# State space input tiles turned during the gated embedding and scaled by the norm afterwards, tables loaded early from ScalarE's queue

## The chip, the cores and the metric

One core of one Trainium2 chip runs the whole kernel in one launch. The metric is device time in microseconds (us); the kernel before is shown by the median of 3 runs and by one profiled execution. TensorE (PE, with its weight loads PEld), VectorE (DVE), ScalarE (ACT), GpSimd (POOL) and SyncE (SP) each work through their own instructions in a fixed order. SP and ScalarE also issue the DMAs of this kernel. The built program counts the landings of these DMAs on eight semaphores in turn, so that an issue also waits until the DMA eight places ahead of it has landed, and what stands behind it on its engine waits too.

## The reference, cut to what matters

Two transformer blocks on x of 512 tokens by 1024 channels. The change lies in the first one, between the gated embedding of layer 0 and the state space mixer of layer 1:

```python
# layer 0, end: gated embedding
gate = sigmoid(rms_norm(x) @ ple_w_gate[0])
x = x + gate * (p[0] @ ple_w_proj[0])
# layer 1, begin: state space mixer over 64 groups of 16 channels, 64 complex states each
h = rms_norm(x, norm_mix[1])                 # x * rsqrt(mean(x*x) + eps) * g
y = s5_mixer(h, ...)                         # input map, complex linear scan over time, output map, + d*h
g_a, g_b = split(gelu(y) @ od_w_glu, 2)
x = x + g_a * sigmoid(g_b)
```

## The kernel before, in words

The kernel keeps x turned, channels on partitions: eight tiles x0 to x7 of 128 channels by 512 tokens. A matmul in fp32 precision is made of three (lines 354 to 356 in `mm_fm`): high half of the weights by high and low half of the input, low half by high half. Weights arrive as 1 MB tiles `raw` (`fetch`, line 310, SP) and are split into `whi` (ScalarE, line 328) and `wlo` (VectorE or GpSimd, line 331).

**The gated embedding** (`ple`, line 872) goes over four weight tiles of two channel tiles each (c = 0 to 3). For each finished tile m it forms the gate (line 933 on ScalarE) and adds to x[m] (lines 934, 935), then calls `done(m)`: here `Rms.add`, a square on ScalarE (line 218) and a sum over tiles. It also multiplies out the projection of layer 1's embedding ahead of time and stores it to HBM (`ahead_of_time`, lines 897 and 902). At the end, `Rms.fin1` sums over channels on TensorE (line 202), forms 1/sqrt on ScalarE and VectorE (`rstd_of`, line 174) and a diagonal matrix (line 189); `Rms.fin2` spreads it over partitions by a matmul with ones (line 196) and ScalarE copies it into a tile `st_r` (line 197). The projection's last two tiles stand between `fin1` and `fin2`.

**The state space mixer** (from line 1192) works on eight units, one per channel tile. It handles the scan in blocks of 4 tokens, so each unit needs its input with channel and token phase on the partitions. For that `drive` (line 1215, VectorE) multiplies x[k] by gain and norm into a tile `h` (two buffers), ScalarE's queue stores it to HBM (`hd`, line 1217), and `lift` reads it back turned, in four DMAs on SP (`up`, line 1223). `load` (line 1210, SP) brings a unit's tables from HBM in six DMAs: `tG` (input map), `tE` (rotations) and `tC` (output map), two buffers each. Then, per unit: `mid` has 8 matmuls `tG` by `up` into two banks (line 1230) and six VectorE products and sums with `tE` (lines 1233 to 1238; called the rotation here); `scan` has two VectorE scans (line 1249) and five or six GpSimd products and sums with `tE` (lines 1256 to 1262; of odd units the difference `xr`, line 1258, is VectorE's); `emit` has 12 matmuls with `tC` (line 1270), a gelu on ScalarE (line 1272), a store to `hd` (line 1273, ScalarE's queue) and four loads that turn it back (`y`, line 1277, SP); `land` splits y into `Gh` (ScalarE, line 291) and `Gl` (VectorE, line 294), the input of the gated linear unit behind it. That unit has eight groups (c = 0 to 3 with two halves s = 1, 0) of 48 matmuls. The group c = 0, s = 1 (`acc0[1]`) is accumulated in the loop, unit by unit; c = 0, s = 0 (`acc0[0]`) stands behind the loop.

A loop over t (line 1293) staggers the units: `load` of t+1, `mid` of t, `scan` of t-1, `land` of t-3, `emit` of t-2, `acc0[1]` of t-4. A scheduler then sets the order of the instructions on each engine by what is ready when; the order in which things stand in a section below is that of the built program. SP's order there is: tables of unit 0, tG of unit 1, lifts of unit 0, tE and tC of unit 1, then all 28 lifts of units 1 to 7, and only then the tables of unit 2.

Of the kernel before, what the change touches and what calls it, by code (L numbers as in the profile page):

```python
# [10 lines left out]
F32 = mybir.dt.float32  # L11
# [7 lines left out]
P = 128  # L19
# [30 lines left out]
def tile_net(ctx: ExitStack, tc: tile.TileContext, a, out):  # L50
# [1138 lines left out]
    rms2 = Rms()  # L1189
    rb2 = ple(0, X, rms, rms2.add, (rms2.fin1, rms2.fin2))  # L1190

    with tc.tile_pool(name="s5r", bufs=1) as rp:
# [5 lines left out]
        class Unit:  # L1198
# [4 lines left out]
            def load(self):  # L1203
                k = self.k
                self.G = rp.tile([P, 4, 256], F32, tag="tG", name=nm("tG"), bufs=2)
                self.E = rp.tile([P, 4, 256], F32, tag="tE", name=nm("tE"), bufs=2)
                self.C = rp.tile([P, 4, 448], F32, tag="tC", name=nm("tC"), bufs=2)
                for t, lo, hi in ((self.G, 0, 256), (self.E, 704, 960), (self.C, 256, 704)):
                    for i in range(2):
                        nc.sync.dma_start(t[:, 2 * i:2 * i + 2, :],  # L1210
                                          tabs[2 * k + i].rearrange("p (q n) -> p q n", q=2)[:, :, lo:hi])

            def drive(self):
                h = rp.tile([P, 4, P], F32, tag="h", name=nm("h"), bufs=2)
                vec.scalar_tensor_tensor(h, x[self.k].rearrange("p (n j) -> p j n", j=4), col("norm_mix", KD + self.k),
                                         rb2.rearrange("p (n j) -> p j n", j=4), op0=ALU.mult, op1=ALU.mult)
                nc.scalar.dma_start(hdr[self.k], h)

            def lift(self):
                self.up = rp.tile([P, 4, P], F32, tag=f"Gh{self.k}", name=nm("up"))  # L1220
                src = hdr[self.k].rearrange("(i c) j n -> j c i n", c=32)
                for b in range(4):
                    nc.sync.dma_start(self.up[32 * b:32 * b + 32], src[3 - b])

            def mid(self):
                k, up = self.k, self.up
# [12 lines left out]
                self.rm = xt_(f"X{'hl'[self.par]}5")  # L1239
                act.copy(self.rm, r4[:, 4 * k:4 * k + 4].unsqueeze(2).to_broadcast([P, 4, P]))  # L1240
                pool.memset(self.rm[:, :, 0:1], 0.0)

            def scan(self):
                k = self.k
                er, ei = self.E[:, :, 0:P], self.E[:, :, P:]
                zr = rp.tile([P, 4, P], F32, tag=f"Gl{k}", name=nm("zr"))
                zi = rp.tile([P, 4, P], F32, tag="zi", name=nm("zi"), bufs=2)
                for z, w in ((zr, self.pv[1]), (zi, self.pv[0])):
                    vec.tensor_tensor_scan(z.rearrange("p i n -> p (i n)"), self.rm.rearrange("p i n -> p (i n)"),
                                           w.rearrange("p i n -> p (i n)"), 0.0, op0=ALU.mult, op1=ALU.add)  # L1250
# [35 lines left out]
        for u in units:  # L1286
            u.drive()
# [537 lines left out]
```

## Time and profile before

| | |
|---|---|
| median of 3 runs | 2817.63 us (2815.61 to 2818.87) |
| the profiled execution | 2815.37 us |
| its span | 2813.6 us |
| PE busy, share of the span | 96% |
| chain that ended last | PE 86%, DVE 6%, POOL 2%, DMA 2%, ACT 2%, issue 2% |
| granted TensorE clock over the span | 0.981 |

Times within the profile are counted from the start of the span. The profiled execution lies 2.3 us below the median. A busy engine is one that executes; TensorE's matmuls overlap, so 96% is not a measure of how full it is. Waits are put down to the work whose semaphore came last.

### The profile page before, as it was taken

Reading aid. Unit: us, or ns where it says so; the run is one execution under the profiler, and the core shown is the slowest. Engines: PE = TensorE matmul, PEld = TensorE weight load, DVE = VectorE, ACT = ScalarE, POOL = GpSimd, SP = SyncE. Lnnn points to the kernel's source line nnn. Section 1 sums busy time; section 2 is a strip of 40 time slices with the busy share of each in tenths; the row PEclk is TensorE's granted clock in tenths of the full one; section 3 lists DMA queues with packets and bytes.
Section 4 is the critical chain, followed back from the end, with each engine's and each line's share of the span. In section 5 each row is a group of like instructions: output and inputs, shape, how many; then the busy total and the mean of one; then the engine's idle time right before and its main releaser. Section 6 shows DMA issues by size and latency. Waiting matters only on the chain.

```text
span 2813.6 us, 35122 instructions
## 1 busy us (share of the span) xinstructions
PE 2709.8 (96%) x14363; PEld 2293.3 (82%) x14363; DVE 1608.2 (57%) x2526; ACT 987.6 (35%) x1287; POOL 671.5 (24%) x590
## 2 busy tenths in 40 slices
PE   8999999999579999999999998999999899999998
PEld 8978888878468888888888887887888778889898
DVE  6456868676664746475333346965478664733335
ACT  5544424345223423244212234333343352431222
POOL 2213045761441000011000035344444321300000
PEclk9999999999789999999999999999999999999999
DMA  5203333433753232223232222232222223222222
GB/s 161 76 31 106 105 111 133 173 118 126 251 173 100 90 100 95 90 95 130 90 105 90 93 87 73 87 100 77 96 81 82 75 90 114 74 98 90 90 92 74
DMA packets 277842, 289.83 MB, mean 103 GB/s; under 512 B 20197, under 2 KB 266951, under 8 KB 277680
## 3 DMA queue, kind: packets, MB, share of 16 engines
q1 hardware_dynamic: 256208, 260.38, 28.9%
q10 hardware_dynamic: 20640, 26.78, 2.7%
q8 instruction: 113, 1.85, 0.3%
q0 software_dynamic: 832, 0.41, 0.1%
q14 instruction: 49, 0.40, 0.0%
HBM read 263.43 MB, written 24.12 MB: 102 GB/s over the span
## 4 chain that ended last, share of the span: by engine, by line
PE 86%; DVE 6%; POOL 2%; issue 2%; DMA 2%; ACT 2%; SPq 0%; POOLq 0%; DVEq 0%; ACTq 0%
PE ps L354 23%; PE ps L355 23%; PE ps L356 23%; PE ps L363 4%; PE ps L365 4%; PE ps L364 4%; DVE ps L1491 1%; PE ps L635 1%; PE ps L1552 1%; PE ps L659 1%; DVE x L287 1%; POOL st_b L263 1%; PE ps L1116 1%; DMA hd<-h 0%; ACT whi L328 0%
## 5 line engine op out<-in xcount | busy, mean ns | idle before, releaser
L328 ACT CAST whi<-raw 128x2048 fp32r<-128x2048 f32 (+2 forms) x216 | 406.2, 1881 | 763.4 <-PE ps L355 608.4
L354 PE MATMUL ps<-Xh,whi 128*128 128x512 f32 (+1 forms) x1472 | 571.3, 389 | 6.8 <-ACT Xh L291 5.1
L356 PE MATMUL ps<-Xh,wlo 128*128 128x512 f32 (+1 forms) x1472 | 566.3, 385 | 3.1 <-DVE wlo L331 3.1
L355 PE MATMUL ps<-Xl,whi 128*128 128x512 f32 (+1 forms) x1472 | 566.7, 385 | 2.7 <-POOL Xl L294 2.7
L331 DVE TENSOR_TENSOR wlo<-raw,whi 128x2048 fp32r<-128x2048 f32 (+2 forms) x167 | 381.0, 2281 | 324.1 <-ACT whi L328 320.2
L331 POOL TENSOR_TENSOR wlo<-raw,whi 128x2048 fp32r<-128x2048 f32 (+1 forms) x49 | 223.5, 4561 | 689.6 <-ACT whi L328 377.7
L354 PEld LDWEIGHTS ps<-Xh,whi 128*128 128x128 f32 x1472 | 278.7, 190 | 65.4 <-ACT Xh L291 5.5
L356 PEld LDWEIGHTS ps<-Xh,wlo 128*128 128x128 f32 x1472 | 279.2, 190 | 60.7 <-DVE wlo L331 4.4
L355 PEld LDWEIGHTS ps<-Xl,whi 128*128 128x128 f32 x1472 | 279.3, 190 | 59.5 <-POOL Xl L294 3.6
L355 PE MATMUL ps<-XBl,whi 128*128 128x512 f32 (+1 forms) x736 | 283.3, 385 | 2.6 <-POOL XBl L294 2.6
L354 PE MATMUL ps<-XBh,whi 128*128 128x512 f32 (+1 forms) x736 | 282.6, 385 | 1.4 <-ACT XBh L291 1.4
L356 PE MATMUL ps<-XBh,wlo 128*128 128x512 f32 (+1 forms) x736 | 282.5, 385 | 0.0
L355 PE MATMUL ps<-Al,whi 128*128 128x512 f32 (+1 forms) x528 | 203.7, 386 | 3.2 <-DVE Al L294 3.2
L354 PE MATMUL ps<-Ah,whi 128*128 128x512 f32 (+1 forms) x528 | 203.6, 388 | 1.2 <-ACT Ah L291 1.2
L356 PE MATMUL ps<-Ah,wlo 128*128 128x512 f32 (+1 forms) x528 | 203.5, 386 | 0.0
L1491 DVE SCALAR_TENSOR_TENSOR ps<-glu,par,ps 128x512 f32<-128x512 f32 x232 | 174.3, 751 | 4.2
L355 PEld LDWEIGHTS ps<-XBl,whi 128*128 128x128 f32 x736 | 139.8, 190 | 31.6 <-POOL XBl L294 3.4
L354 PEld LDWEIGHTS ps<-XBh,whi 128*128 128x128 f32 x736 | 139.4, 190 | 29.3 <-ACT XBh L291 1.8
L356 PEld LDWEIGHTS ps<-XBh,wlo 128*128 128x128 f32 x736 | 139.8, 190 | 28.0
L220 POOL TENSOR_TENSOR st_a<-st_a,st_q 128x512 f32<-128x512 f32 x25 | 44.3, 1770 | 487.9 <-ACT st_q L218 487.8
L363 PE MATMUL ps<-whi,Xh 128*128 128x256 f32 (+1 forms) x512 | 147.7, 289 | 0.7 <-ACT z L597 0.4
L364 PE MATMUL ps<-wlo,Xh 128*128 128x256 f32 (+1 forms) x512 | 145.0, 284 | 0.0
(472 smaller groups left out, 4869.7 us busy)
## 6 DMA issues: line engine op xcount, KB each, us to landing
raw<-in_ffn_w_up_dram SPq DMA_DIRECT2D x66, 1024.0 KB, 5.1
raw<-in_w_in_dram SPq DMA_DIRECT2D x40, 1024.0 KB, 5.2
raw<-in_ffn_w_down_dram SPq DMA_DIRECT2D x32, 1024.0 KB, 4.9
raw<-in_ffn_w_gate_dram SPq DMA_DIRECT2D x22, 1024.0 KB, 5.2
tab<-tabs ACTq DMA_DIRECT2D x16, 960.0 KB, 4.1
raw<-in_ffn_w_down_dram SPq DMA_DIRECT2D x16, 768.0 KB, 4.2
raw<-in_ev_w_in_dram SPq DMA_DIRECT2D x8, 1024.0 KB, 5.2
raw<-in_ple_w_gate_dram SPq DMA_DIRECT2D x8, 1024.0 KB, 4.9
```

What stands on the lines that cost most here:

```text
L220: eng.tensor_tensor(self.acc, self.acc, sq, op=ALU.add)
L263: eng.tensor_tensor(self.sq[:, c], self.sq[:, c], q[:, c], op=ALU.add)
L287: vec.tensor_tensor(xm, xm, self.rb[:, c], op=ALU.mult)
L328: cp = act.copy(hi, rv)
L331: lo.tensor_tensor(lw, rv, hi.bitcast(F32), op=ALU.subtract)
L354: pe.matmul(acc, wh[j][:, s], X.h[k], start=start and t == 0, stop=False)
L355: pe.matmul(acc, wh[j][:, s], X.l[k], start=False, stop=False)
L356: pe.matmul(acc, wl[j][:, s], X.h[k], start=False, stop=stop and t == len(ks) - 1)
L363: pe.matmul(acc, X.h[k][:, s], wh[j], start=start and t == 0, stop=False)
L364: pe.matmul(acc, X.h[k][:, s], wl[j], start=False, stop=False)
L365: pe.matmul(acc, X.l[k][:, s], wh[j], start=False, stop=stop and t == len(ks) - 1)
L1491: vec.scalar_tensor_tensor(x[m] if t == 30 else acc, u[:, t:t + T], col("ck", t * KD + m), acc, op0=ALU.mult, op1=ALU.add)
```

## The change

What it does:

- `turn_in(k)` runs from `ple`'s `done(m)`, as soon as x[m] is final: ScalarE multiplies x[k] by the gain alone (line 1220 of the new file), ScalarE's queue stores h, SP lifts it into `up`. The norm is applied afterwards: `phases` spreads the diagonal as `rbt`, one value per partition phase and block of tokens, in four copies of 32 partitions (line 1321), and `norm` multiplies `up` by it in place (line 1228: unit 0 on VectorE, units 1 to 7 on GpSimd). `drive` on VectorE and the copy into `st_r` are gone.
- The tables go out on ScalarE's queue instead of SP's (line 1204), as separate loads of G, E and C, E with three buffers; tC is 416 columns wide instead of 448. The built program has G, E and C of units 0 and 1 and E of unit 2 at the very beginning of the embedding, on ScalarE around that stage's first square root and weight split. The pool that holds them is opened ahead of the embedding.
- In the loop, the input matmuls (`feed`) run one unit ahead; the rotation is `spin`. Unit 7's six products and sums behind the scan go to VectorE.
- The eight steps of the group `acc0[0]`, one for each unit, are given places in the loop (three at t = 8, three at t = 9, one each at t = 10 and 11) instead of behind it.

```diff
-    rms2 = Rms()
-    rb2 = ple(0, X, rms, rms2.add, (rms2.fin1, rms2.fin2))
-    with tc.tile_pool(name="s5r", bufs=1) as rp:
+    with tc.tile_pool(name="s5e", bufs=1) as ep, ExitStack() as late:
+        rms2 = Rms()
...
-            def load(self):
-                self.G = rp.tile([P, 4, 256], F32, tag="tG", name=nm("tG"), bufs=2)
-                self.E = rp.tile([P, 4, 256], F32, tag="tE", name=nm("tE"), bufs=2)
-                self.C = rp.tile([P, 4, 448], F32, tag="tC", name=nm("tC"), bufs=2)
...
-                        nc.sync.dma_start(t[:, 2 * i:2 * i + 2, :],
-                                          tabs[2 * k + i].rearrange("p (q n) -> p q n", q=2)[:, :, lo:hi])
-            def drive(self):
-                vec.scalar_tensor_tensor(h, x[self.k].rearrange("p (n j) -> p j n", j=4), col("norm_mix", KD + self.k),
-                                         rb2.rearrange("p (n j) -> p j n", j=4), op0=ALU.mult, op1=ALU.mult)
...
+            def table(self, tag, lo, hi, bufs):
+                t = ep.tile([P, 4, hi - lo], F32, tag=tag, name=nm(tag), bufs=bufs)
+                for i in range(2):
+                    nc.scalar.dma_start(t[:, 2 * i:2 * i + 2, :],
+                                        tabs[2 * self.k + i].rearrange("p (q n) -> p q n", q=2)[:, :, lo:hi])
+                return t
+            def load_g(self):
+                self.G = self.table("tG", 0, 256, 2)
+            def load_e(self):
+                self.E = self.table("tE", 704, 960, 3)
+            def load_c(self):
+                self.C = self.table("tC", 288, 704, 2)
+            def turn_in(self):
+                k = self.k
+                h = ep.tile([P, 4, P], F32, tag="h", name=nm("h"), bufs=2)
+                act.activation(h, x[k].rearrange("p (n j) -> p j n", j=4), AF.Copy, scale=col("norm_mix", KD + k))
+                nc.scalar.dma_start(hdr[k], h)
+                self.up = ep.tile([P, 4, P], F32, tag=f"Gh{k}", name=nm("up"))
+                src = hdr[k].rearrange("(i c) j n -> j c i n", c=32)
+                for b in range(4):
+                    nc.sync.dma_start(self.up[32 * b:32 * b + 32], src[3 - b])
+            def norm(self, eng):
+                eng.tensor_tensor(self.up, self.up, rbt.unsqueeze(1).to_broadcast([P, 4, P]), op=ALU.mult)
...
+        def ready(m):
+            rms2.add(m)
+            units[m].turn_in()
+            if m == 1:
+                units[0].load_g()
+                units[0].load_e()
...
+        def phases():
+            b = bank((P, P, 4))
+            pe.matmul(b.rearrange("p n j -> p (n j)"), ones, rms2.dg.rearrange("p i t -> p (i t)"),
+                      start=True, stop=True)
+            for j in range(4):
+                r = slice(32 * j, 32 * j + 32)
+                (vec.tensor_copy if j % 2 else act.copy)(rbt[r], b[r, :, 3 - j])
+        ple(0, X, rms, ready, (rms2.fin1, phases))
...
+        units[0].norm(vec)
+        units[0].feed()
+        units[2].load_g()
+        for k in range(1, 5):
+            units[k].norm(pool)
         for t in range(KD + 4):
+            if at(t + 1):
+                at(t + 1).feed()
+            if at(t + 3):
+                at(t + 3).load_g()
...
+            if t > 1 and at(t + 1):
+                at(t + 1).load_e()
+            if t == KD:
+                acc0[0] = [bank() for _ in range(2)]
+                mm_fm(acc0[1], w0s[1], G, [4], start=False, stop=False, js=[4])
+                for k in range(3):
+                    mm_fm(acc0[0], w0s[0], G, [k], start=k == 0, stop=False, js=[k])
+            if at(t - 2):
+                at(t - 2).emit()
+            if t and at(t):
+                at(t).load_c()
...
-        acc0[0] = [bank() for _ in range(2)]
-        mm_fm(acc0[0], w0s[0], G, K8)
```

**Place 1**: ScalarE at the end of the embedding (`st_q` are the squares of x6 and x7, `pjd` the stores of the projection, `rs` the square root, `st_r` the spread norm, `h` the tile that is turned). Before:

```order
L218 ACTIVATE st_q_6459<-x_78 128x512
...
L218 ACTIVATE st_q_6467<-x_79 128x512
...
L902 DMA pjd<-Xl_864_6516 128x512
L902 DMA pjd<-Xl_865_6517 128x512
L174 ACT_TABLE_LOAD
L174 ACTIVATE rs_6543<-rv_6541 128x4
...
L197 COPY st_r_6574<-ps_6575 128x512
L1217 DMA hd_2535<-h_6591 128x512
```

With the change:

```order
L218 ACTIVATE st_q_6529<-x_78 128x512
L1220 ACTIVATE h_6532<-x_78,par 128x512
L1220 ACTIVATE h_6548<-x_79,par 128x512
L1221 DMA hd_2541<-h_6532 128x512
L218 ACTIVATE st_q_6545<-x_79 128x512
L1221 DMA hd_2542<-h_6548 128x512
...
L902 DMA pjd<-Xl_887_6603 128x512
L174 ACT_TABLE_LOAD
L174 ACTIVATE rs_6629<-rv_6627 128x4
...
L1321 COPY rbt<-ps_6660 32x128 x2
L1204 DMA tG_6684<-tab_2523 128x2x256
```

The last two tiles' turning stands ahead of the square root, between the squares; the last `pjd` store ahead of it is the eighth DMA, over SP and ScalarE, behind the store of unit 7's h, and so waits for that one to land.

**Place 2**: ScalarE in one round of the loop (`g` is a gelu, `Gh` the high half of a turned y, `s` the scan's multiplier). Before:

```order
L1272 ACTIVATE g_7027<-ps_7014 128x512
L1273 DMA hd_2538<-g_7027 128x512
L1240 COPY s_1035_7138<-r_2518 128x512
L1272 ACTIVATE g_7106<-ps_7093 128x512
L1273 DMA hd_2539<-g_7106 128x512
L291 CAST Gh_7089<-y_7030 128x512
```

With the change:

```order
L291 CAST Gh_7000<-y_6901 128x512
L1237 COPY s_1002_7020<-r_2518 128x512
L1204 DMA tE_7031<-tab_2531 128x2x256
L1204 DMA tE_7031<-tab_2532 128x2x256
L1287 ACTIVATE g_7047<-ps_7034 128x512
L1204 DMA tC_7055<-tab_2529 128x2x416
L1288 DMA hd_2538<-g_7047 128x512
L1204 DMA tC_7055<-tab_2530 128x2x416
L291 CAST Gh_7075<-y_6974 128x512
```

The tables' issues now stand between ScalarE's own work: the load of E for unit 6 stands behind the cast of unit 1's turned y, which waits for y to land.

**Place 3**: TensorE ahead of the output matmuls of unit 6 (`tC` rows), with `ps_7222` and `ps_7223` the banks of `acc0[0]`. With the change:

```order
L1285 MATMUL ps_7170<-xi_7063,tC_7055 128x128
L354 MATMUL ps_7222<-Gh_6926,whi_6806 128x512
L355 MATMUL ps_7222<-Gl_6927,whi_6806 128x512
L356 MATMUL ps_7222<-Gh_6926,wlo_6807 128x512
L354 MATMUL ps_7223<-Gh_6926,whi_6806 128x512
...
L356 MATMUL ps_7223<-Gh_7075,wlo_6807 128x512
L1285 MATMUL ps_7248<-up_6535,tC_7131 128x128
L1285 MATMUL ps_7248<-xr_7138,tC_7131 128x128
```

Before, no matmul of `acc0[0]` stood ahead of unit 6's output matmuls. Counted over the whole loop, 48 of the 384 matmuls of the gated linear unit stand ahead of the last output matmul of unit 7 with the change, and 34 before.

## Rows read from the trace of the kernel before

**Rows 1.** The page's second part: the span in 40 slices of 70.3 us, each digit TensorE's busy share in tenths.

```profile
PE   8999999999579999999999998999999899999998
```

**Rows 2.** Stretches of the span: length, busy time of each engine with its instructions (PE, PEld, DVE, ACT, POOL), granted TensorE clock, busy share of the DMA engines, GB/s.

```profile
690.00:714.00 24.00, 23.35 (x105) 18.79 (x105) 15.06 (x23) 14.87 (x24) 2.92 (x8) 1.00 0.47 154
714.00:736.00 22.00, 4.49 (x18) 3.49 (x16) 8.52 (x8) 0.81 (x2) 0.00 (x0) 0.61 0.94 307
736.00:757.00 21.00, 8.67 (x42) 8.44 (x42) 16.93 (x21) 4.32 (x4) 15.79 (x13) 0.51 0.56 166
757.00:784.00 27.00, 14.69 (x104) 13.02 (x102) 19.16 (x26) 4.88 (x8) 17.75 (x23) 0.80 0.90 276
784.00:806.00 22.00, 17.93 (x106) 15.70 (x107) 15.18 (x20) 3.05 (x5) 18.14 (x20) 0.81 0.86 252
806.00:822.00 16.00, 13.29 (x94) 11.72 (x94) 12.69 (x14) 4.08 (x8) 8.68 (x9) 0.95 0.42 126
822.00:836.00 14.00, 14.00 (x62) 11.05 (x61) 2.27 (x4) 5.47 (x8) 0.00 (x0) 1.00 0.37 113
```

**Rows 3.** ScalarE in order of time at the end of the embedding: start, us, engine, line, operation, out<-in, [idle before it and who ended it]. ACTq is its queue of DMA issues.

```profile
708.27 0.63 ACT L218 ACTIVATE st_q<-x 128x512 f32<-128x512 f32 x1 [0.76 <-DVE st_a L220]
...
710.27 1.28 ACT L174 ACT_TABLE_LOAD   x1 [0.41 <-ACT Xl L897]
711.56 0.20 ACT L174 ACTIVATE rs<-rv 128x4 f32<-128x4 f32 x1
...
713.70 0.33 ACTq L902 DMA_DIRECT2D pjd<-st_b  x1
...
714.78 0.58 ACT L197 COPY st_r<-ps 128x512 f32<-128x512 f32 x1 [0.55 <-PE ps L196]
```

**Rows 4.** VectorE in order of time, columns as in rows 3: the last multiplication by the norm, the begin of the rotations of units 0, 2, 3, 4 and 7, and the last scan of unit 0.

```profile
735.26 1.12 DVE L1215 SCALAR_TENSOR_TENSOR h<-x,par,st_r 128x512 f32<-128x512 f32 x1 [0.94 <-DMA hd<-h]
736.30 0.69 DVE L1233 TENSOR_TENSOR s<-tE,ps 128x512 f32<-128x512 f32 x1
...
741.01 1.20 DVE L1249 TENSOR_TENSOR_SCAN zr<-s,ps 128x512 f32<-128x512 f32 x1
...
756.06 0.68 DVE L1233 TENSOR_TENSOR s<-tE,ps 128x512 f32<-128x512 f32 x1
...
761.88 0.66 DVE L1233 TENSOR_TENSOR s<-tE,ps 128x512 f32<-128x512 f32 x1
...
775.97 0.69 DVE L1233 TENSOR_TENSOR s<-tE,ps 128x512 f32<-128x512 f32 x1 [0.26 <-DMA tE<-tab]
...
807.23 0.69 DVE L1233 TENSOR_TENSOR s<-tE,ps 128x512 f32<-128x512 f32 x1 [5.87 <-PE ps L1230]
```

**Rows 5.** SP's queue in order of time: the lifts of units 1 to 7 and the first tables of unit 2.

```profile
729.63 19.08 SPq L1223 DMA_DIRECT2D up<-hd  x28
748.81 1.18 SPq L1210 DMA_DIRECT2D tG<-tab  x2
```

**Rows 6.** DMAs of the loop, 740 to 820 us: queue q1 (SP) and q10 (ScalarE) with packets, MB and busy share of the 16 engines, then the issues: KB each and median us from issue to landing.

```profile
q1 hardware_dynamic: 17445, 15.86, 68.0%
q10 hardware_dynamic: 1008, 1.84, 6.1%
...
tE<-tab SPq DMA_DIRECT2D x12, 256.0 KB, 4.5
hd<-g ACTq DMA_DIRECT2D x7, 256.0 KB, 4.5
y<-hd SPq DMA_DIRECT2D x28, 64.0 KB, 4.2
```

**Rows 7.** Landing times, shortest, median and longest, of the stores of h (line 1217), and of the tables (line 1210).

```profile
DMA to landing us min/median/max: 2.0/4.5/6.1
...
DMA to landing us min/median/max: 3.1/5.0/10.4
```

**Rows 8.** GpSimd in order of time: first and last instruction of unit 5 (five products and sums) and of unit 6 (six).

```profile
792.78 1.27 POOL L1256 TENSOR_TENSOR s<-tE,zr 128x512 f32<-128x512 f32 x1 [2.20 <-DVE zr L1249]
...
799.53 1.27 POOL L1256 TENSOR_TENSOR s<-tE,zr 128x512 f32<-128x512 f32 x1
...
806.13 1.27 POOL L1262 TENSOR_TENSOR xi<-v,v 128x512 f32<-128x512 f32 x1
```

**Rows 9.** Line 1258, the difference `xr`, on either engine: duration in ns, shortest, median and longest.

```profile
L1258 POOL TENSOR_TENSOR xr<-s,s x4: 1262/1271/1280, 748.1 to 804.9; 128x512 f32<-128x512 f32 x4
L1258 DVE TENSOR_TENSOR xr<-s,s x4: 1029/1733/1739, 754.4 to 816.5; 128x512 f32<-128x512 f32 x4
```

**Rows 10.** TensorE in order of time: the input matmuls of unit 0 (two banks), and the first and last pair of the output matmuls of unit 7.

```profile
727.63 3.75 PE L1230 MATMUL ps<-up,tG 128*128 128x128 f32 x16 [12.89 <-DMA up<-hd]
...
819.38 0.49 PE L1270 MATMUL ps<-xi,tC 128*128 128x128 f32 x2 [0.63 <-POOL xi L1262]
...
821.50 0.39 PE L1270 MATMUL ps<-xi,tC 128*128 128x128 f32 x2
```

**Rows 11.** ScalarE in order of time where the early loads and the first tiles' turning go: a copy of 32 partitions, and a weight split of the embedding with the idle time before it.

```profile
639.89 0.26 ACT L1123 COPY tabs<-ps 32x128 f32<-32x128 f32 x1
...
665.70 1.90 ACT L328 CAST whi<-raw 128x2048 fp32r<-128x2048 f32 x1 [8.40 <-issue]
```

More of the change, by code (lines that the diff above doesn't have):

```diff
@@ L1229, in mid @@
                     for i in range(4):
-                        pe.matmul(pv[z][:, i, :], self.G[:, i, P * z:P * z + P], up[:, i, :], start=True, stop=True)
+                        pe.matmul(self.pv[z][:, i, :], self.G[:, i, P * z:P * z + P], self.up[:, i, :],
+                                  start=True, stop=True)
+                self.rm = xt_(f"X{'hl'[self.par]}5")
+                act.copy(self.rm, r4[:, 4 * self.k:4 * self.k + 4].unsqueeze(2).to_broadcast([P, 4, P]))
+                pool.memset(self.rm[:, :, 0:1], 0.0)
@@ L1280, in land, with at @@
                 k = self.k
[L1281 removed]
+                G.h[k] = ep.tile([P, T], F32R, tag=f"Gh{k}", name=nm("Gh"))
+                G.l[k] = rp.tile([P, T], F32R, tag=f"Gl{k}", name=nm("Gl"))
                 split(G.h[k], G.l[k], self.y.rearrange("p r n -> p (r n)"))
         units = [Unit(k) for k in range(KD)]
[L1285 to L1291 removed]
+        def ready(m):
[4 more added lines that the diff above has]
+                units[0].load_e()
+            elif m == 3:
+                units[1].load_g()
+                units[1].load_e()
+            elif m == 5:
+                units[0].load_c()
+                units[2].load_e()
+        def phases():
+            b = bank((P, P, 4))
+            pe.matmul(b.rearrange("p n j -> p (n j)"), ones, rms2.dg.rearrange("p i t -> p (i t)"),
+                      start=True, stop=True)
+            for j in range(4):
+                r = slice(32 * j, 32 * j + 32)
+                (vec.tensor_copy if j % 2 else act.copy)(rbt[r], b[r, :, 3 - j])
+        rbt = ep.tile([P, P], F32, name="rbt")
+        ple(0, X, rms, ready, (rms2.fin1, phases))
+        rp = late.enter_context(tc.tile_pool(name="s5r", bufs=1))
+        def at(k):
+            return units[k] if 0 <= k < KD else None
+        units[0].norm(vec)
[3 more added lines that the diff above has]
+            units[k].norm(pool)
         acc0, w0s = {}, {}
         for t in range(KD + 4):
[L1294 to L1299 removed]
+            if at(t + 1):
+                at(t + 1).feed()
+            if at(t + 3):
+                at(t + 3).load_g()
+            if at(t):
+                at(t).spin()
+                if at(t - 1) and t % 2 == 0:
+                    at(t - 1).real(vec)
             if t == 2:
@@ L1303, in tile_net @@
                 acc0[1] = [bank() for _ in range(2)]
-            if 0 <= t - 3 < KD:
-                units[t - 3].land()
-            if 0 <= t - 2 < KD:
-                units[t - 2].emit()
-            if 0 <= t - 4 < KD:
-                k = t - 4
-                mm_fm(acc0[1], w0s[1], G, [k], start=k == 0, stop=k == KD - 1, js=[k])
+            if t > 1 and at(t + 1):
[9 more added lines that the diff above has]
+                at(t).load_c()
+            if at(t):
+                at(t).scan()
+                if at(t + 5):
+                    at(t + 5).norm(pool)
+            if at(t - 3):
+                at(t - 3).land()
+            if at(t - 4):
+                k = t - 4
+                if t != KD:
+                    mm_fm(acc0[1], w0s[1], G, [k], start=k == 0, stop=k == KD - 1, js=[k])
+                if t == KD + 1:
+                    for j in (3, 4, 5):
+                        mm_fm(acc0[0], w0s[0], G, [j], start=False, stop=False, js=[j])
+                elif t > KD + 1:
+                    mm_fm(acc0[0], w0s[0], G, [k], start=False, stop=k == KD - 1, js=[k])
             if t == KD:
```

65 lines of the change are left out of this document (25 added, 40 removed).

## The prediction

> **What bounds the kernel now.** I looked first at the slices of the span: TensorE is at 0.8 or more everywhere but in two slices, at 0.5 and 0.7, the eleventh and twelfth, 703 to 844 us [rows 1]. So what the change can win lies in the state space stage. The view of stretches says how that stage goes [rows 2]: until 714 TensorE is full (23.35 of 24 us); from 714 to 736 it works 4.49 of 22 us, while the DMA engines are busy 0.94 of the time; then it rises slowly, and from 822 it is full again (14.00 of 14). From 736 to 806 no engine is full: VectorE 16.93 of 21, GpSimd 15.79 of 21, DMA 0.90 in the middle stretch. It is a chain through several engines, and I read it in order of time, in four parts: the start, the interval from unit to unit, the tail of the last unit, and the work that is laid into the loop.
>
> Start: the spread norm is copied at 714.78 [rows 3], then the first input matmul waits 12.89 us for the lifted h and begins at 727.63 [rows 10]; the rotation of unit 0 comes at 736.30 only, because VectorE works off the eight multiplications by the norm first, and those wait for the stores of h that free their buffer (0.94 us ahead of the last) [rows 4]. Interval: the rotations run from 736.30 to 807.23, seven intervals of 10.13 us on average; the waits that show are tables (0.26 us at 775.97) and an input matmul (5.87 at 807.23) [rows 4]. The tables are late since SP issues them behind 19.08 us of lifts [rows 5]. Tail: from the last rotation to the end of unit 7's output matmuls, 821.50 + 0.39, it is 14.7 us [rows 4, 10].
>
> **The start.** x6 and x7 are turned by ScalarE between the squares and the square root. Two multiplications of 128x512 have as nearest rows the square, 0.63, and VectorE's multiplication, 1.12 [rows 3, 4]; I take 0.8, nearer the row of the same engine. The last square stands at 708.27 behind a gap of 0.76 [rows 3], and an issue is 0.33: it moves by 1.6 + 0.33 - 0.76 = 1.2 us, ends at 710.1, and h of unit 7 is issued by 710.4. The last store of the projection ahead of the square root waits for that landing, 4.5 us (2.0 to 6.1) [rows 7]: 714.9. The table load of 1.28 follows [rows 3], so the square root begins at 716.2 instead of 711.56, 4.65 us later. What hangs on it before takes until the copy at 714.78 [rows 3], now 719.4; two copies of 32 partitions on either engine at 0.26 [rows 11] give 720.0. The norm of unit 0 on VectorE reads two operands in SBUF; the nearest row is its `xr`, 1.03 to 1.73 [rows 9]; at 1.03 it ends at 721.0. The rotation needs the first bank, half of 3.75 us [rows 10]: **722.9 instead of 736.30, 13.4 us earlier.** The landing alone moves this by -2.5 to +1.6.
>
> What I set at nothing here: the loads of the first tables and the turning of x0 to x5 lie in the embedding, where ScalarE stands idle for 8.40 us ahead of one weight split [rows 11] and is busy 14.87 of 24 us at the end, beside a full TensorE [rows 2]; if that cover is gone, a split comes late, which is the third rival below. The lifts of h on SP stand between the fetches of weights; unit 0's are five tiles ahead of their use. The seven norms on GpSimd stand ahead of its products: at 1.31 us (a sixth of unit 6's 7.87, from 799.53 to 806.13 + 1.27 [rows 8]) they run to 729.2, and the products of unit 0 are ready at 722.9 + 5.9 = 728.8 (rotation and scans of unit 0 took 736.30 to 742.2 [rows 4]). That is 0.4 us, once. Unit 7's h lands at 714.9, its four lifts take 0.68 each to issue [rows 5] and 4.2 to land [rows 6]: 721.8, well ahead of its norm at 728.
>
> **The interval.** Three bounds. GpSimd keeps 39 products and sums for units 0 to 6, 39 x 1.31 / 7 = 7.3 us a unit. DMA: the two queues moved 17.70 MB between 740 and 820 us at 74.1% [rows 6], 59 us of the engines' time, 7.4 us a unit if the loop's traffic stays. The ring of waits: the load of E stands behind the cast of the turned y five units back. From E: rotation and scans 5.9, GpSimd 7.9, output matmuls 2.5 (819.38 to 821.9 [rows 10]), gelu, cast and the copy for the scan 0.6 each (as the copy in [rows 3]), store 4.5, four issues 2.7, y 4.2, two issues at 0.59 [rows 5], E 4.5 [rows 6]: 35.2 us over five units, 7.0. With the longest landings (10.4 for E, 6.1 for the store and for y [rows 7]) it is 44.6, 8.9. So nothing forces 10.13 any longer, unless the DMA engines do. I take **8.3 us**: between 7.4 and 8.9, in the upper half, since the DMA engines were at 0.86 to 0.90 there [rows 2] and landings are then nearer the long end. 7 x (10.13 - 8.3) = **12.8 us earlier**; bounds 0 (10.13 stays) and 19.1 (7.4).
>
> The clock that TensorE was granted while it idled, 0.51 to 0.61, then 0.80 [rows 2], costs it something in every short burst; a fuller TensorE may get it back sooner. I don't add to the sum for it.
>
> **The tail.** Before, 14.7 us: rotation and scans 5.9, output matmuls 2.5, and 6.3 for the products, on GpSimd but for one. Now six on VectorE. At the `xr` row's shortest, 1.03 [rows 9], 6.2 us: 0.1 us earlier. The bounds are 0.69, as in the rotation (4.1, -2.2 us) [rows 4], and 1.73 (10.4, +4.1). I take the shortest, since GpSimd, at 7.3 us a unit, ends about when these begin. The Trainium skill ("GPSIMD Engine Reference", section "Key points") says that GpSimd shares its SBUF interfaces with VectorE and contends with VectorE's instructions that have two SBUF inputs; the two values 1.03 and 1.73 look like that, and with GpSimd still at work the tail would go by 1.73.
>
> **Work laid into the loop.** 48 instead of 34 matmuls of the gated linear unit stand ahead of unit 7's last output matmul. If those 14 run in waits of TensorE they are gone from the full stretch behind, where 62 matmuls took 14.00 us [rows 2]: 14 x 0.226 = **3.2 us**, between 0 and 3.2. It needs the next group's first matmuls to fill the wait for unit 7's y; in the built order they do.
>
> **Sum** against the profiled execution of 2815.37: -13.4 - 12.8 - 0.1 - 3.2 = -29.5, 2785.9. The median of the runs lies 2.3 above the profiled execution: **2788.2 us**. Unit 7's output matmuls would end at 722.9 + 7 x 8.3 + 14.6 = 795.6 instead of 821.9.
>
> **Rivals.** All against the median.
>
> *The transfers keep the interval.* The tables leave SP's queue, but the bytes stay, and they pass the same 16 engines, busy 0.86 to 0.90 in the loop [rows 2]. For it: 68.0% of the engines' time was SP's queue alone [rows 6]; tables wait for landings on ScalarE now, between its gelus and casts. Against it: 7.4 us a unit of transfers is below 10.13, and the lifts are out of the way. At 10.13 the second term is gone: -16.7, 2800.9 us. The Trainium skill ("DMA: Bandwidth & Descriptors", section "Issuing engines are not separate DMA queues") says that DMAs issued by different engines run on the same 16 engines and interleave, so that a second issuer saves only issue time; by it the move of the tables alone would leave the interval as it is. The trace agrees so far as q1 and q10 add up to one busy share. Chance 0.19.
>
> *The embedding pays.* Turning on ScalarE's queue holds copies that free TensorE's banks. For it: a store there waits for landings of up to 6.1 us [rows 7]; against it: ScalarE's idle time [rows 2, 11]. One such landing in TensorE's way: -23.4, 2794.2. Chance 0.05.
>
> *The change does not bring the input ahead.* If SP's lifts sit behind fetches that wait for buffers, unit 0 starts as late as before, at 727.63 [rows 10], rotation at 729.5: -6.8 for the start, -22.9, 2794.7. Chance 0.04.
>
> *Slower: E late every round.* The load of E is issued by ScalarE behind a cast that waits for y; if the ring takes longer than its parts, each unit waits for its table. Unit 3 to unit 4 took 761.88 to 775.97 = 14.09 us with E late [rows 4]. With that each time: 7 x 3.96 = +27.7 - 16.7 = +11.0, 2828.6. It decides from 10.13 + 16.7 / 7 = 12.5 us a unit, where the ring would have to be 62 us long, 18 over its slow value. Chance 0.04.
>
> **Numbers.** My forecast has the remaining 0.68. The low end, 2779, is the interval of 7.4 (6.3 less) with half of the earliest landing; the high end, 2805, is the first rival with the slow tail (+4.1). That leaves out the slower rival and the ends of two cases. What measurements of this kernel can tell from no change is about 0.2%, 5.6 us; every case but the last is faster by more: faster 0.95, same 0.02, slower 0.03.
>
> **What would show it.** First multiplication of a rotation near 723 and square root near 716, with the last store of the projection waiting for the store of h; rotations 8.3 us apart; GpSimd with few gaps from 721 on; unit 7's products at 1.03; its last output matmul near 796; TensorE full up to 714. I am wrong where E or y ends most waits of VectorE's rotations and the interval stays at 10, or where TensorE has gaps between 640 and 714 that it had not.

## The result, and the profile after

The change takes 2794.42 us (median of 4 runs, 2790.44 to 2797.59) against 2818.25 us of the kernel before on the same chip: ratio 0.9913, 95% interval 0.9898 to 0.9927, or 24.5 us with 20.6 to 28.7. Forecast were 29.5 us less, 2788.2 us. The profiled execution takes 2794.66 us with a span of 2792.9.

TensorE executes 14363 matmuls in both kernels. The 4600th starts behind the stage, at 863.49 us before and 839.83 after; the stage is thus 23.7 us shorter by the trace, 5.8 less than forecast. (Of these 23.7, this pair of profiles loses 3.0 again, almost all of it between 1692 and 1942 us, in code that the change does not touch: there the granted clock is 0.91 from 1690 to 1708 and 0.89 from 1908 to 1933, where the same code had 1.00 and 0.93 before. Why it was granted less stays open.)

The stretches of the changed kernel, columns as in [rows 2]:

```profile
690.00:714.00 24.00, 22.08 (x98) 18.12 (x97) 13.52 (x17) 18.02 (x25) 2.67 (x4) 0.95 0.79 255
714.00:720.00 6.00, 3.82 (x13) 2.47 (x13) 2.79 (x9) 1.94 (x6) 1.22 (x5) 0.90 0.61 196
720.00:736.00 16.00, 9.07 (x70) 8.26 (x69) 15.11 (x22) 4.42 (x4) 15.51 (x14) 0.88 0.52 158
736.00:757.00 21.00, 13.65 (x78) 13.08 (x77) 13.24 (x13) 1.81 (x3) 12.54 (x15) 0.74 0.58 169
757.00:784.00 27.00, 20.58 (x122) 18.51 (x122) 20.98 (x27) 5.40 (x9) 22.25 (x25) 0.83 0.81 237
784.00:801.00 17.00, 15.28 (x97) 13.23 (x98) 14.31 (x20) 3.38 (x6) 9.47 (x12) 1.00 0.56 172
801.00:817.00 16.00, 16.00 (x74) 13.12 (x73) 4.70 (x8) 6.27 (x11) 0.00 (x0) 1.00 0.43 117
```

The 22 us in which TensorE worked 4.49 are gone, and it is full from 801 instead of 822. Between 736 and 757 it is still idle a third of the time, with VectorE at 13.24 and GpSimd at 12.54 of 21 us: everyone waits for someone there. VectorE in order of time, columns as in [rows 3]:

```profile
720.89 0.69 DVE L1244 TENSOR_TENSOR s<-tE,ps 128x512 f32<-128x512 f32 x1 [1.27 <-PE ps L1234]
...
743.62 1.73 DVE L1277 TENSOR_TENSOR xr<-s,s 128x512 f32<-128x512 f32 x1 [7.43 <-POOL s L1265]
745.28 3.35 DVE L331 TENSOR_TENSOR wlo<-raw,whi 128x2048 fp32r<-128x2048 f32 x1
748.55 1.21 DVE L1256 TENSOR_TENSOR_SCAN zr<-s,ps 128x512 f32<-128x512 f32 x1
...
750.79 0.66 DVE L1244 TENSOR_TENSOR s<-tE,ps 128x512 f32<-128x512 f32 x1
...
758.25 0.69 DVE L1244 TENSOR_TENSOR s<-tE,ps 128x512 f32<-128x512 f32 x1 [1.58 <-DMA tE<-tab]
...
767.30 1.73 DVE L1277 TENSOR_TENSOR xr<-s,s 128x512 f32<-128x512 f32 x1 [4.76 <-POOL s L1265]
...
786.37 0.66 DVE L1244 TENSOR_TENSOR s<-tE,ps 128x512 f32<-128x512 f32 x1
...
789.34 1.64 DVE L294 TENSOR_TENSOR Gl<-y,Gh 128x512 fp32r<-128x512 f32 x1
...
793.74 0.66 DVE L1266 TENSOR_TENSOR s<-tE,zi 128x512 f32<-128x512 f32 x1
...
795.53 0.68 DVE L1277 TENSOR_TENSOR xr<-s,s 128x512 f32<-128x512 f32 x1
```

Against [rows 4] the first rotation stands at 720.89 instead of 736.30, the last at 786.37 instead of 807.23: 9.35 us apart on average, where 8.3 were forecast and 10.13 were before. E is waited for once, 1.58 us. The long waits are the two ahead of `xr`, the difference of odd units that VectorE forms from GpSimd's products; unit 2's scans and unit 3's rotation (750.79) stand behind the first one. GpSimd, which makes VectorE wait, waits itself:

```profile
718.97 9.13 POOL L1228 TENSOR_TENSOR up<-up,rbt 128x512 f32<-128x512 f32 x7 [1.98 <-DVE rbt L1321]
728.07 1.27 POOL L1266 TENSOR_TENSOR s<-tE,zi 128x512 f32<-128x512 f32 x1
...
734.20 1.26 POOL L1274 TENSOR_TENSOR xi<-s,s 128x512 f32<-128x512 f32 x1
...
739.60 0.10 POOL L1262 MEMSET xr<- 128x4 f32 x1 [4.09 <-PE ps L1285]
...
739.88 1.27 POOL L1266 TENSOR_TENSOR s<-tE,zi 128x512 f32<-128x512 f32 x1
...
750.80 0.10 POOL L1262 MEMSET xr<- 128x4 f32 x1 [4.33 <-PE ps L1285]
...
763.12 0.10 POOL L1262 MEMSET xr<- 128x4 f32 x1 [4.34 <-PE ps L1285]
```

The row to see is the one at 739.60. `xr` and `xi` have two buffers, and their column 0 is set to zero for each unit (lines 1262, 1263). In the built order the zero column of unit 2 stands in GpSimd's queue ahead of unit 1's products (739.88), and it may be written only when the output matmuls of unit 0 have read that buffer. So a write of 0.10 us holds products that do not need it. The matmuls that it waits for end late:

```profile
734.29 0.79 PE L1285 MATMUL ps<-xr,tC 128*128 128x128 f32 x2 [4.56 <-POOL xr L1277]
735.52 0.79 PE L1285 MATMUL ps<-xi,tC 128*128 128x128 f32 x2 [0.43 <-POOL s L1238]
736.11 0.63 PE L1285 MATMUL ps<-up,tC 128*128 128x128 f32 x2
...
739.32 0.39 PE L1285 MATMUL ps<-xi,tC 128*128 128x128 f32 x2
```

For three rounds it goes like this: GpSimd finishes a unit, TensorE reads it, and only then GpSimd begins the next. The chain that ended last runs through these rounds, in turn on GpSimd and on TensorE, until 767. With the input earlier the writes wait 13.4 us in all. Before the change the same writes waited 6.3 us, and VectorE waited for GpSimd ahead of `xr` there too; two rows of each engine from the trace of before:

```profile
754.40 1.74 DVE L1258 TENSOR_TENSOR xr<-s,s 128x512 f32<-128x512 f32 x1 [2.71 <-POOL s L1256]
...
772.16 1.73 DVE L1258 TENSOR_TENSOR xr<-s,s 128x512 f32<-128x512 f32 x1 [4.39 <-POOL s L1256]
```

```profile
758.68 0.10 POOL L1253 MEMSET xr<- 128x4 f32 x1 [1.41 <-PE ps L1270]
...
810.41 0.10 POOL L1253 MEMSET xr<- 128x4 f32 x1 [3.00 <-PE ps L1270]
```

### The profile page after: what moved, and what is told of

Read it like the earlier page. It is cut to its first block, busy times and chain, and to the rows that moved or that the text cites. A ratio compares the mean times of both kernels' runs of the same rounds, so it can differ in the third digit from the quotient of the medians.

```text
span 2792.9 us, 35139 instructions
## 1 busy us (share of the span) xinstructions
PE 2711.1 (97%) x14363; PEld 2293.5 (82%) x14363; DVE 1602.1 (57%) x2526; ACT 995.5 (36%) x1296; POOL 672.4 (24%) x592
## 4 chain that ended last, share of the span: by engine, by line
PE 87%; DVE 5%; POOL 3%; issue 2%; ACT 2%; DMA 1%; SPq 0%; POOLq 0%; ACTq 0%; DVEq 0%
PE ps L354 23%; PE ps L355 23%; PE ps L356 23%; PE ps L363 4%; PE ps L365 4%; PE ps L364 4%; DVE ps L1553 1%; PE ps L1285 1%; PE ps L635 1%; PE ps L1614 1%; POOL st_b L263 1%; PE ps L659 1%; DVE x L287 1%; PE ps L1116 1%; ACT whi L328 0%
## 5 line engine op out<-in xcount | busy, mean ns | idle before, releaser
L354 PEld LDWEIGHTS ps<-XBh,whi 128*128 128x128 f32 x736 | 139.2, 190 | 29.5 <-ACT XBh L291 1.8
```

The lines of the kernel that those rows point to most:

```text
L354: pe.matmul(acc, wh[j][:, s], X.h[k], start=start and t == 0, stop=False)
```

## Experiments

Each kernel is the change with the edit shown. In the table, "rotation" is the start of the first one, "zero waits" the idle time of GpSimd ahead of the writes of zero columns, and "4600th" the start of that matmul. Ratios are to the kernel before on the same chip; their intervals are some +-0.15%, 4 us, so smaller differences between two edits rest on the trace, one profiled execution of each. The runs come from several chips, on which the kernel before had medians from 2817.83 to 2820.57, so a difference of two medians also holds up to 2.7 us of the chips; "to the change" is the difference of the two ratios, in us of 2818.25. An edit also changes what is ready when, and with it the order that the scheduler builds (e3, e4, e11): what an edit costs is not only what it says.

| | median us | ratio, interval | to the change | rotation | interval us | zero waits | 4600th |
|---|---|---|---|---|---|---|---|
| before | 2818.25 | |  | 736.30 | 10.13 | 6.3 | 863.5 |
| the change | 2794.42 | 0.9913 (0.9898, 0.9927) |  | 720.89 | 9.35 | 13.4 | 839.8 |
| e1 | 2787.16 | 0.9891 (0.9878, 0.9905) | -6.2 | 721.77 | 8.39 | 0 | 835.2 |
| e2 | 2793.92 | 0.9916 (0.9902, 0.9929) | +0.8 | 722.94 | 9.47 | 13.5 | 840.6 |
| e3 | 2798.41 | 0.9935 (0.9922, 0.9949) | +6.2 | 720.21 | 10.03 | 13.4 | 842.4 |
| e4 | 2790.65 | 0.9901 (0.9887, 0.9914) | -3.4 | 720.66 | 8.83 | 10.3 | 835.9 |
| e5 | 2793.91 | 0.9908 (0.9895, 0.9922) | -1.4 | 728.29 | 8.40 | 6.4 | 840.2 |
| e6 | 2799.28 | 0.9924 (0.9912, 0.9937) | +3.1 | 722.19 | 9.24 | 13.5 | 846.2 |
| e7 | 2799.04 | 0.9924 (0.9911, 0.9936) | +3.1 | 720.71 | 9.32 | 13.4 | 846.0 |
| e8 | 2784.34 | 0.9871 (0.9854, 0.9888) | -11.8 | 719.41 | 8.09 | 0 | 829.5 |
| e9 | 2793.05 | 0.9905 (0.9892, 0.9919) | -2.3 | 728.06 | 8.36 | 0 | 840.1 |
| e10 | 2801.38 | 0.9928 (0.9914, 0.9942) | +4.2 | 725.75 | 9.61 | 0 | 845.6 |
| e11 | 2790.45 | 0.9894 (0.9880, 0.9907) | -5.4 | 725.06 | 8.45 | 0 | 837.7 |
| e12 | 2781.43 | 0.9864 (0.9847, 0.9880) | -13.8 | 718.89 | 8.17 | 0 | 829.5 |

**e1, zero columns written once.**

```diff
-                self.xr = rp.tile([P, 4, P + 1], F32, tag="xr", name=nm("xr"), bufs=2)
-                self.xi = rp.tile([P, 4, P + 1], F32, tag="xi", name=nm("xi"), bufs=2)
-                pool.memset(self.xr[:, :, 0:1], 0.0)
-                pool.memset(self.xi[:, :, 0:1], 0.0)
+                self.xr, self.xi = xs[self.par]     # two fixed pairs, column 0 set ahead of the loop
```

> xr and xi become two fixed tiles each whose zero column is written once ahead of the loop; everything else stays as in the change. Theory 1 (GpSimd's queue): in the change the writing of the zero column for unit k+2 stands in GpSimd's queue ahead of the products of unit k+1 and waits for the output matmuls of unit k, 4.1 + 4.3 + 4.3 us in the first rounds, and VectorE waits 7.4 + 4.8 us behind it for xr of odd units. Then these waits go, the interval between rotations falls from 9.35 to 7.8 +- 0.4 us and the kernel is 8 to 13 us faster than the change (about 2784 against 2794.4). Theory 2 (transfers): the interval is kept by the DMA engines, busy 0.81 from 757 to 784; GpSimd's gaps move to other places and the time stays within 2 us. Theory 3 (the ring over E and the cast of y): as theory 2.

It took 7.3 us off the change's median, 6.2 by the ratios, a little less than theory 1's 8 to 13, and the stage is 4.6 us shorter by the trace; theories 2 and 3 gave 2 at most. The intervals of the two ratios overlap; the waits that are gone are read from the trace. GpSimd of e1, around what was the first wait, and VectorE's `xr` of unit 1:

```profile
735.43 1.29 POOL L1263 TENSOR_TENSOR s<-tE,zi 128x512 f32<-128x512 f32 x1
...
745.43 1.27 POOL L1262 TENSOR_TENSOR s<-tE,zr 128x512 f32<-128x512 f32 x1 [3.36 <-DVE zr L1256]
```

```profile
739.20 1.75 DVE L1274 TENSOR_TENSOR xr<-s,s 128x512 f32<-128x512 f32 x1 [1.81 <-POOL s L1262]
...
755.61 0.69 DVE L1244 TENSOR_TENSOR s<-tE,ps 128x512 f32<-128x512 f32 x1 [3.34 <-DMA tE<-tab]
```

Unit 1's products follow at 735.43 instead of 739.88, and VectorE waits 1.81 instead of 7.43 us. The interval fell to 8.39, not to 7.4 to 8.2: GpSimd now waits for VectorE's scans (8.6 us in all), and E, which was late once by 1.58 us, is late by 3.34.

**e2, no tables after the first.** `load_g`, `load_e` and `load_c` of later units take the tiles of units 0 to 2 instead of a load.

> Tables are loaded for units 0 and 1 (E also for unit 2) and used again for all others, so the loads of the later units' tables, 20 issues on ScalarE of 256 KB or 416 KB, are left out, and the output is another. Theory 1 (GpSimd's queue): the interval stays at 9.35, at best 1.6 us less in all, the one wait for E that shows on VectorE: 0 to 3 us faster. Theory 2 (transfers): interval 7.4 to 8.2, 8 to 13 us faster. Theory 3 (ring over E): interval 7.4, more than 10 us faster.

The time stayed (0.9916 against 0.9913), though 34 issues are gone (the 20 of the expectation was a miscount). The stretches of e2 show how little is transferred; the last two columns are the DMA engines' share and GB/s:

```profile
720.00:740.00 20.00, 13.95 (x89) 13.50 (x90) 16.39 (x24) 2.10 (x3) 16.56 (x14) 0.80 0.02 8
740.00:760.00 20.00, 10.74 (x61) 9.87 (x60) 14.26 (x14) 4.63 (x6) 13.94 (x16) 0.76 0.33 105
760.00:780.00 20.00, 16.42 (x91) 15.00 (x92) 13.80 (x19) 3.47 (x6) 15.21 (x16) 0.76 0.12 41
```

In the same stretches the change has the engines at 0.44, 0.74 and 0.73. With 0.02 to 0.33 the interval is 9.47. So neither the transfers nor the ring over E bound the changed loop.

**e3, later tables on SP.**

```diff
-                    nc.scalar.dma_start(t[:, 2 * i:2 * i + 2, :],
+                    (nc.sync if self.k > 1 else nc.scalar).dma_start(t[:, 2 * i:2 * i + 2, :],
```

> The tables of units 2 to 7 go out on SP's queue, those of units 0 and 1 stay on ScalarE's. That is the queue's part of the change undone. Theory 1 (GpSimd's queue): SP has no lifts in the loop any more, so E comes in time on either queue: within 3 us of the change. Rival (the queue is what pays in the interval): interval back to 10.1, 5 us or more slower.

4.0 us slower by the medians, 6.2 by the ratios, 2.6 by the trace; the intervals overlap, so the time does not decide between the two expectations. The interval between rotations is 10.03, near the rival's 10.1. But VectorE does not wait for E here; its waits ahead of `xr` add up to 17.8 us (three) instead of 12.2. The third, 3.63 us at 782.13, comes with the built order: unit 5's `xr` stands ahead of unit 6's rotation (783.80), where in the change it stands behind it (778.51, `xr` at 783.03) and waits for nothing. Up to unit 5 the rotations come as in the change (771.78 against 771.20). So what this run shows is the order that came with the other queue, not a late table.

**e4, turned after the embedding.** `turn_in` of all units called behind `ple`.

> All eight turn_in calls stand behind the embedding instead of inside it; the norm still comes afterwards. That is the start's part of the change undone. My sum: h of unit 0 is stored from about 715 on, 4.5 us to land, lifts 2.7 + 4.2: input matmuls at 727, first rotation at 728 to 729 instead of 720.9, and the later units' lifts keep the first rounds longer: 7 to 12 us slower than the change (2802 to 2806). Rival (the embedding pays for the turning, and the start brings nothing): within 2 us.

This missed: 3.8 us faster (3.4 by the ratios). The edit did not do what I wrote. The scheduler still turns x0 to x5 inside the embedding, since they are ready; only x6 and x7 moved, behind the square root (712.40 instead of 714.06), and TensorE idles 0.6 instead of 2.6 us between 640 and 714. One norm less stands ahead of unit 0's products on GpSimd, which begin at 726.1 instead of 728.1, and the zero waits fall to 10.3 us. How the 3.8 us divide between these three is not shown. The stage is 3.9 us shorter by the trace.

**e5, the norm first again.** VectorE's multiplication by gain and norm behind `fin2`, as in the kernel before, and no norms on GpSimd.

```diff
-                act.activation(h, x[k].rearrange(...), AF.Copy, scale=col("norm_mix", KD + k))
+                vec.scalar_tensor_tensor(h, x[k].rearrange(...), col("norm_mix", KD + k), rb2.rearrange(...),
+                                         op0=ALU.mult, op1=ALU.mult)
```

> The input is multiplied by the norm before it is stored, by VectorE, as in the kernel before (spread norm copied, eight multiplications by gain and norm, then store and lifts behind the embedding); the norms on GpSimd are gone with it; tables, loop order and unit 7 stay as in the change. e4_turned_after did not test this, since the built order still turned x0 to x5 inside the embedding. Theory 1 with my sum for the start: first rotation at 734 to 736 instead of 720.9; GpSimd is free of 9 us of norms, so the first rounds run closer: 10 to 15 us slower than the change (2804 to 2809). Rival (the early tables, not the turned input, make the start): first rotation near 722, within 3 us of the change.

Theory 1's number fell: no slower (0.9908). The first rotation is 7.4 us later, not 14, because the built order now puts it between the multiplications. VectorE and GpSimd of e5:

```profile
728.29 0.68 DVE L1245 TENSOR_TENSOR s<-tE,ps 128x512 f32<-128x512 f32 x1
...
762.92 0.69 DVE L1245 TENSOR_TENSOR s<-tE,ps 128x512 f32<-128x512 f32 x1 [4.44 <-DMA tE<-tab]
```

```profile
734.23 1.27 POOL L1267 TENSOR_TENSOR s<-tE,zi 128x512 f32<-128x512 f32 x1 [19.26 <-DMA tG<-tab]
...
750.67 0.10 POOL L1263 MEMSET xr<- 128x4 f32 x1 [2.35 <-PE ps L1286]
...
751.64 1.27 POOL L1266 TENSOR_TENSOR s<-tE,zr 128x512 f32<-128x512 f32 x1 [0.58 <-DVE zr L1257]
```

GpSimd begins 6.2 us later than in the change (734.23 against 728.07), and at unit 2 it is level (751.64 against 751.34). The lead that the turned input brings is used up by the zero waits.

**e9, e1 and e5 together**, was made to test that:

> e1 and e5 together: zero columns written once, and the norm ahead of the store. e5 was as fast as the change although its first rotation came 7.4 us later (728.3) and GpSimd's first product 6.2 us later (734.2); by unit 2 GpSimd was level (751.6 against 751.3), because the change lost the lead in GpSimd's waits and VectorE's behind them. Theory 1 then says that with the waits gone the lead is kept: 4 to 6 us slower than e1 (2791 to 2793). Rival (the lead is lost in any case, to tables or TensorE): within 2 us of e1 (2785 to 2789).

5.9 us slower than e1 by the medians, 3.9 by the ratios (with intervals that overlap), 4.9 by the trace. Where GpSimd doesn't wait for the zero columns, the turned input is worth about 5 us; in the change it is worth nothing that shows. In e5 the zero columns cost nothing either (e9 is as e5).

**e10, e3 and e5 together.**

> e5 with the tables of units 2 to 7 on SP's queue (e3). In e5 SP issues lifts from 719.7 to 748.2; tables behind them come late, as before the change (unit 2's rotation 14 us behind unit 1's there). If the queue of the tables matters only while lifts fill SP: rotations of units 2 to 4 come 5 to 10 us later than in e5 and the kernel is 5 to 10 us slower than e5 (2799 to 2804), clearly more than the 4 us of e3. Rival (the early tables of units 0 to 2 are enough): 4 us or less.

7.5 us slower than e5 by the medians, 5.6 by the ratios, 5.4 by the trace, as expected. Of the rotations only unit 2's comes 5 to 10 us later (747.73 against 740.98); unit 3's is 1.0 us later, unit 4's 3.6 earlier. SP and TensorE of e10:

```profile
717.24 19.26 SPq L1226 DMA_DIRECT2D up<-hd  x32
736.60 2.49 SPq L1204 DMA_DIRECT2D tG<-tab  x4
```

```profile
739.87 6.64 PE L1235 MATMUL ps<-up,tG 128*128 128x128 f32 x32 [12.96 <-DMA tG<-tab]
```

G of unit 2 is issued behind 19.26 us of lifts, and TensorE waits 12.96 us for it, where it waits 4.12 in e5. That is what the queue costs where lifts fill SP. That the move of the tables pays mainly there is not shown: e3, without these lifts, costs 6.2 us by the ratios, no less than the 5.6 here. The Trainium skill ("DMA: Bandwidth & Descriptors", section "Issuing engines are not separate DMA queues") says that a second issuer saves only the time of issuing, which is usually small beside the DMA. The trace agrees on what is saved, but it is not small here: 19.26 us of issues stand ahead of that table.

**e11, the first tables behind the embedding.** Loads of units 0 and 1 and E of unit 2 called behind `ple`, in the pool that is opened there.

> The change with the first tables (G, E and C of units 0 and 1, E of unit 2) loaded behind the embedding, still on ScalarE's queue. Twelve issues, 3.4 MB, at 3.35 us per MB some 8 us of the DMA engines for what unit 0 and 1 need first. First rotation 4 to 6 us later, 725 to 727. Theory 1: GpSimd is held by the norms until 728 and then by its waits, so most of that is eaten: 1 to 4 us slower than the change (2795.5 to 2798.5). Rival (the early tables carry the start): 5 us or more slower.

The sign missed: 4.0 us faster (5.4 by the ratios, 2.2 by the trace), though the first rotation is 4.2 us later, as expected. GpSimd of e11:

```profile
742.94 1.59 POOL L1274 TENSOR_TENSOR xi<-s,s 128x512 f32<-128x512 f32 x1
744.51 0.10 POOL L1262 MEMSET xr<- 128x4 f32 x1
...
744.62 1.27 POOL L1265 TENSOR_TENSOR s<-tE,zr 128x512 f32<-128x512 f32 x1
```

With other ready times the scheduler put the zero column of unit 2 behind unit 1's products (742.94), where the output matmuls have long read the buffer: zero waits 0, unit 2's products at 744.62 instead of 751.34. This is the cause shown a second time, without an edit to it: a later start with the better order wins. It also says that the early tables are worth less than that order.

**e6 and e7, the tail and the work laid into the loop.** e6 sets `eng = pool` for unit 7; e7 puts `mm_fm(acc0[0], w0s[0], G, K8)` behind the loop.

> Unit 7's products and sums go back to GpSimd (the difference xr stays on VectorE, as before). In the change the six take 4.2 us on VectorE (0.68 each, not the 1.03 of my sum). On GpSimd they end about 6.4 us behind the scans: 2 us slower than the change, at most 4 (2796 to 2798). Rival (another wait covers the tail): within 1 us.

> The eight steps of the group acc0[0] stand behind the loop again. My sum: the matmuls ahead of unit 7's last output matmul fall by 14 or so, 14 x 0.226 = 3.2 us slower (2797 to 2798). Rival (they only change places with others): within 1 us.

They cost 4.9 and 4.6 us by the medians, both 3.1 by the ratios, as expected, but 6.4 and 6.1 by the trace, more than expected. In e6, GpSimd begins unit 7's products about when VectorE did (793.95 against 793.74), but it takes until 800.6 instead of 798.0, and the output matmuls end at 807.9 instead of 801.6. The larger part comes over VectorE and TensorE: `xr` waits for GpSimd, the low half of a turned y (`Gl`) stands behind `xr`, and the gated linear unit waits for it; VectorE and TensorE of e6:

```profile
797.71 1.73 DVE L1277 TENSOR_TENSOR xr<-s,s 128x512 f32<-128x512 f32 x1 [3.37 <-POOL s L1265]
```

```profile
801.17 0.80 PE L355 MATMUL ps<-Gl,whi 128*128 128x512 f32 x1 [4.56 <-DVE Gl L294]
```

In e7 42 matmuls stand ahead of the last output matmul instead of 48, 6 fewer and not 14, and still it ends later, at 806.2. TensorE of e7:

```profile
791.64 0.78 PE L1285 MATMUL ps<-xr,tC 128*128 128x128 f32 x2 [3.98 <-POOL xr L1277]
792.88 0.80 PE L1285 MATMUL ps<-xi,tC 128*128 128x128 f32 x2 [0.45 <-POOL xi L1263]
```

Without the laid-in matmuls TensorE idles 3.98 us there, and the output matmuls behind it take 0.8 and then 0.63 us a pair until 798, instead of 0.39.

**e8 and e12, towards a better version.** e8 is e1 and e4; e12 is e8 with `real(vec)` of units 1, 3 and 5 behind the next unit's scans instead of ahead.

> e1 and e4 together. e4 gave 3.8 us on the change: the square root came 1.7 us earlier since x6 and x7 are turned behind it, and six norms instead of seven stand ahead of unit 0's products on GpSimd (1.2 us). e1 gave 7.3 us by taking away GpSimd's waits. If the two are separate: 2783.5 +- 1.5. If e4's gain came through the same waits of GpSimd (9.5 us of them instead of 12.8): 2786 to 2788, no better than e1.

> e8 (zero columns written once, x6 and x7 turned behind the square root) with xr of units 1, 3 and 5 standing behind the scans of the next unit in VectorE's queue instead of ahead of them. In e8 VectorE waited 2.0 us for GpSimd ahead of the first such xr, and GpSimd 5.1 us for scans (two times) that stood behind it. If these waits stand on the path: GpSimd's 5.1 us shrink and the kernel is 1 to 4 us faster than e8 (about 2782 at e8's 2784.3). Rival: the output matmuls of odd units come 2.4 us later, as long as two scans, and give it back: within 1 us.

e8 (2784.3) is near the sum of the two: 10.1 us by the medians, where they gave 7.3 and 3.8, and 10.3 by the trace, where they gave 4.6 and 3.9. e12 is the fastest, 2781.43 us, 0.9864 (0.9847 to 0.9880), 13 us below the change. Its 2.9 us on e8 lie within the intervals, and the 4600th matmul starts at the same 829.5 in both: that step is not shown.

## Why the forecast was near in the sum and wrong in a step

The measured gain, 24.5 us, lies 5 us below the forecast. Part of the nearness is luck: the start brought 2.0 us more than forecast and so covers some of the 7.3 that are missing in the interval.

- **Start**: -13.4 forecast, -15.4 measured. The square root came at 714.06, not 716.2: the store of unit 7's h, issued at 709.90, landed after 2.1 us, not the 4.5 that I took, before ScalarE was through with its own copies (712.33), so the wait that I put in does not show. The norm on VectorE took 0.69, not 1.03 us. The norms on GpSimd, which I put at 0.4 us, cost more: unit 0's products could begin with the scan that ends at 725.7 and begin at 728.07. ScalarE of the changed kernel:

```profile
709.77 0.62 ACT L218 ACTIVATE st_q<-x 128x512 f32<-128x512 f32 x1
709.90 0.33 ACTq L1221 DMA_DIRECT2D hd<-h  x1
...
712.77 1.28 ACT L174 ACT_TABLE_LOAD   x1 [0.43 <-ACT Xl L897]
714.06 0.21 ACT L174 ACTIVATE rs<-rv 128x4 f32<-128x4 f32 x1
```

- **The interval** is the step that failed: -12.8 forecast, 7 x (10.13 - 9.35) = -5.5 measured. I bounded it by GpSimd's work, by the transfers and by the ring over E, and took 8.3 as if GpSimd ran through "with few gaps from 721 on". It waits 13.4 us, by the place of a zero write in its queue. That write stands in the kernel before with 6.3 us of waits, and I listed what the change adds to GpSimd's queue without asking what in it already waited for TensorE. My reading of before named as waits of VectorE a table (0.26) and an input matmul (5.87) and left out those for GpSimd ahead of `xr` (2.71, 4.39 and 1.41). With the zero writes away (e1) the interval is 8.39, near the 8.3, but not by the reasons of the forecast: GpSimd still waits 8.6 us there, for scans.
- **Tail**: -0.1 forecast, 15.2 - 14.7 = +0.5 measured. Unit 7's six products took 0.68 each, not 1.03; GpSimd had ended by then. Beside a working GpSimd `xr` took 1.73, as the Trainium skill's rule on the shared interfaces ("GPSIMD Engine Reference", section "Key points") and [rows 9] have it. What that saved went elsewhere: VectorE forms two low halves of y in this stretch (1.64 at 789.34, 0.68 at 796.73), and when the last product ends at 798.0, TensorE is at the gated linear unit until 798.5. The sum had neither. e6 shows that the term is not independent: left on GpSimd, the tail is 21.0 us, by what stands behind `xr` on VectorE.
- **Work laid into the loop**: -3.2 forecast. The last output matmul ends 20.3 us earlier and the 4600th matmul starts 23.7 earlier, so 3.4 lie behind the loop, as forecast; taken out alone it costs 6.1 of the stage by the trace (e7), though only 6 matmuls move, so it pays by more than their number.
- **Rivals**: transfers as the bound and E late every round are refuted for the changed kernel by e2 and by the one wait of 1.58 us. The input did come ahead. The embedding pays little: TensorE idles 2.6 us between 640 and 714, 1.4 before.
- **The range**: by its own terms the low end is 2788.2 - 6.3 - 1.3 = 2780.6, not 2779.
- **The parts**: undone one at a time they cost 2.6 (e3), 0.4 (e5), 6.4 (e6), 6.1 (e7) and -2.2 us (e11) by the trace, 13.3 of 23.7. No run puts the rest down to one part.

## What to carry to other kernels

When a stage's input is brought forward, look on each in-order queue for small instructions that wait on the engine behind them (buffer resets, constant columns): they stand between one unit and the next, and the lead is lost there. Write constant columns once per buffer. Gains of single edits need not add up through such a queue: the turned input was worth about 0 with the zero waits and 5 us without them (e1 and e4 did add up).

## What was not expected of the hardware

- In the changed kernel's stretch with a granted clock of 0.74 (736 to 757) the clock stands at its lower level, 1.2 GHz, for part of the time, behind waits of TensorE such as the 4.56 us ahead of 734.29; most of the pairs of output matmuls of units 0 and 1 take 0.63 us there, where those at the upper level, 2.4 GHz (784 to 801, 1.00), take 0.39. The chain that ended last passes through such matmuls in three rounds (twenty matmuls in 4.20, 4.65 and 4.49 us), where the 24 of unit 7 took 2.85. TensorE's idle time thus comes back on the path, by way of the matmuls that GpSimd waits for.
- A GpSimd product took 3.33 instead of 1.27 us beside VectorE's 128x2048 split (2.47 us, e11, at 745.85); before the change there is one of 3.33 us too, at 744.85, beside a split of 2.30.
